# Depthwise convolution: the shifted copies of a chunk's quarters by DMA within SBUF instead of products with the identity

## The chip, the cores and the metric

One core of a Trainium2 chip runs the whole program. The metric is the device time of one execution in microseconds, as the median of several runs; lower is better. Engine names are those of the profile: PE (matmuls) and PEld (its weight loads), DVE, ACT, POOL, and SP, whose queue issues nearly all DMAs.

## The reference

Two layers on 256 tokens of 2048 channels in float32. Layer 0 mixes tokens by a state-space model, layer 1 by a convolution module; each mixer is followed by a SwiGLU FFN, and each half ends in a residual and a LayerNorm. The change lies in the convolution module of layer 1:

```python
CONV_WIDTH = 31
def conv_mixer(u, w_pw1, w_dw, b_dw, g_norm, b_norm, w_pw2):
    d = u.shape[-1]
    ab = u @ w_pw1
    v = ab[..., :d] * jax.nn.sigmoid(ab[..., d:])
    v = lax.conv_general_dilated(            # causal, one filter of 31 taps per channel
        v, w_dw[:, None, :], window_strides=(1,), padding=((CONV_WIDTH - 1, 0),),
        dimension_numbers=('NWC', 'WIO', 'NWC'), feature_group_count=d) + b_dw
    v = layer_norm(v, g_norm, b_norm)
    return jax.nn.silu(v) @ w_pw2
```

## The kernel before, in words

Activations lie with channels on the 128 partitions, in 16 chunks of 128 channels. The first product of the module (`cv_w_pw1`) runs in 8 panels, i = 0 to 7; a panel makes two chunks, `ch = 2 * i` and `2 * i + 1`. A panel has 4 units. A unit is 512 rows of the weights, loaded by SP into one of 4 `raw` buffers (L572, two DMAs for a unit of these panels), split by ACT (`whi`, L816) and DVE (`wlo`, L817) into one of 2 pairs of buffers, and used by 24 matmuls of 128x512 (L870; in the last panel 48 of 128x256, L874). The same 4 `raw` buffers also take the weights of the conditioning projection (`rawa`, L670), 0.6 of a 1 MB load for each unit, which DVE multiplies and adds (`adaacc`, L685).

The order around the products is set by two counters. `later.put(n, fn)` traces `fn` n units later, ahead of that unit's matmuls; `turning.put` does the same for the transposes that follow a panel. The units of the panels are units 1 to 32 of the count used here: panel i has 4i+1 to 4i+4. The framework then orders each engine's queue by its own estimate of what is ready, so the order on the chip is near, but not always equal to, the order of tracing. Each engine runs its queue strictly in order.

A panel's gated output is turned back to channels-on-partitions by 4 transposes (`turned`, L886) in unit 4i+6, that is in the second unit of the next panel. Panel 0 (made by another routine) and panel 7 need no such turn. Then `conv_in(i)` runs:

- ACT copies each chunk behind 30 zeros into one of two `pad` tiles (L1497).
- POOL makes the tap weights `lw` (L1502), three buffers, one for each chunk.
- `conv_spread` (L1513): the 128 channels of a chunk are four quarters q of 32. For each quarter, 4 products with 32 columns of the identity put it on the partitions 32j to 32j+31, moved by j = 0..3 positions, into one PSUM bank of 284 columns; ACT (q even, L1515) or DVE (q odd, L1517) copies the bank into `vs`. So `vs[32j + c, q, t]` is channel 32q + c at position t + j.
- `conv_out` (L1523): 8 tap groups x 4 quarters of products of `lw` (128 x 32) with `vs` (128 x 256) give a chunk's convolution; DVE moves it to `V` with the bias (L1527, L1532), and the sums for the LayerNorm are kept (`cstats.add`, L750 to L761).

The spread of chunk k (0 or 1) of a panel is put off by 1 + k units, its `conv_out` by 2 + k. After panel 7 all that was put off is worked off (`later.flush()`, L1540), the LayerNorm's sums are finished (L776 to L795), and the second product (`cv_w_pw2`) starts.

Of the kernel before, what the change touches and what calls it, by code (L numbers as in the profile page):

```python
# [11 lines left out]
F32 = mybir.dt.float32  # L12
# [7 lines left out]
P = 128  # L20
# [125 lines left out]
def bc(ap, axis, n):  # L146

    a = ap.unsqueeze(axis)
    sh = list(a.shape)
    sh[axis] = n  # L150
    return a.broadcast_to(sh)
# [344 lines left out]
def kernel(  # L496
# [9 lines left out]
    nc = tc.nc  # L506
# [6 lines left out]
    def aux(name):  # L513
        return auxp.tile([P, 512], F32, tag="aux", name=name)
# [81 lines left out]
    later, turning = Later(), Later()  # L596
# [839 lines left out]
    with mctx:  # L1436
# [46 lines left out]
        cp = cvctx.enter_context(tc.tile_pool(name="cv", bufs=1, reuse_waits="tile"))  # L1483
        V = cp.tile([P, NCH, SEQ], F32, name="V")
        LP = WIDTH - 1 + SEQ + 1
        LS = 4 * CONV_G - 4 + SEQ
# [7 lines left out]
        def conv_in(i, t):  # L1494
            p = pad[i % 2]
            for k in range(2):
                nc.scalar.copy(out=p[:, k, WIDTH - 1:LP - 1].rearrange("p (c t) -> p t c", t=2), in_=t[:, k].rearrange("p (t c) -> p t c", t=2))  # L1497
            for k in range(2):
                ch = 2 * i + k
                vs = cp.tile([P, 4, LS], F32, tag="vs", name="vs", bufs=3)  # L1500
                lw = cp.tile([P, 4, CONV_G, 32], F32, tag="lw", name="lw", bufs=3)
                nc.gpsimd.tensor_tensor(  # L1502
                    out=lw, in0=fold32.unsqueeze(1).unsqueeze(1).broadcast_to([P, 4, CONV_G, 32]),
                    in1=bc(wtap[:, :, 4 * ch:4 * ch + 4].rearrange("p g q -> p q g"), 3, 32), op=MUL)
                later.put(1 + k, lambda z=p[:, k], vs=vs: conv_spread(z, vs))
                later.put(2 + k, lambda ch=ch, lw=lw, vs=vs: conv_out(ch, vs, lw))

        def conv_spread(z, vs):

            for q in range(4):  # L1510
                b = aux("spread")[:, :LS]
                for j in range(4):
                    nc.tensor.matmul(b[32 * j:32 * j + 32, :], ident[:, 32 * q:32 * q + 32], z[:, j:j + LS], start=True, stop=True)  # L1513
                if q % 2 == 0:
                    nc.scalar.copy(out=vs[:, q], in_=b)  # L1515
                else:
                    nc.vector.tensor_copy(out=vs[:, q], in_=b)  # L1517

        def conv_out(ch, vs, lw):
            acc = aux("conv")[:, :SEQ]  # L1520
            for g in range(CONV_G):
                for q in range(4):
                    nc.tensor.matmul(  # L1523
                        acc[32 * q:32 * q + 32, :], lw[:, q, g, :], vs[:, q, 4 * g:4 * g + SEQ], start=g == 0, stop=g == CONV_G - 1)
            o, a = V[:, ch].rearrange("p (t c) -> p c t", t=2), acc.rearrange("p (c t) -> p c t", t=2)
            if ch < 2:
                nc.vector.tensor_scalar(out=o, in0=a, scalar1=cb_col[:, ch:ch + 1], scalar2=None, op0=ADD)  # L1527
                if ch == 1:
                    later.put(1, lambda: cstats.begin(V[:, 0:2]))
                    later.put(1, lambda: cstats.add(0, V[:, 0:2]))  # L1530
                return
            nc.vector.scalar_tensor_tensor(  # L1532
                out=o, in0=a, scalar=cb_col[:, ch:ch + 1], in1=cstats.shift.rearrange("p (t c) -> p c t", t=2), op0=ADD, op1=SUB)
            if ch % 2 == 1:
                cstats.add(ch // 2, V[:, ch - 1:ch + 1])

        for i in range(8):
            gated(cv_w_pw1[0], 256 * i, D, sp, lambda t, i=i: conv_in(i, t), entry if i == 0 else None, wp=wp, wide=i < 7,
                  ahead=(cv_w_pw2[0], [(0, 512)]) if i == 7 else None)
# [87 lines left out]
```

## Time and profile before

| | |
|---|---|
| median of 3 runs | 2364.49 us (2362.25 to 2364.72) |
| the profiled execution's own time | 2360.99 us |
| its span | 2359.0 us |
| mean granted TensorE clock | 0.989 |
| PE busy | 2278.7 us (97%) |
| DVE busy | 1647.2 us (70%) |
| ACT busy | 1024.3 us (43%) |
| POOL busy | 235.8 us (10%) |
| DMA, mean | 243 GB/s |

The span is the stretch that the profile covers; the times quoted are counted from its start. The panels of `cv_w_pw1` that follow panel 0 run from about 1207 to 1452 us, and the flush ends at about 1470 us. A row of a timeline gives start, duration, engine, line, operation, output and inputs, and a count when several were merged; in square brackets is how long the engine was idle before and what ended that. A row of the chain gives start, duration and work; the chain is followed back from the last instruction to what released each step. A row of stretches gives, for each engine, busy us and number of instructions, then PE's granted clock, the busy share of the 16 DMA engines and their rate in GB/s.

### The profile page before, as it was taken

To read this page: it belongs to the slowest core of one execution; us is meant where nothing else is said; L and a number is where in the kernel's file an instruction comes from. 1 tells how busy PE (TensorE), PEld (TensorE's weight loads), DVE (VectorE), ACT (ScalarE), POOL (GpSimd) and SP (SyncE) were. 2 spreads that over 40 slices of the span, in tenths; PEclk is the share of its full clock that TensorE was granted. 3 is DMA by queue.
4 is the path that set the end of the run, shared out by engine and by line. 5 is a ranking of instruction groups with operands and counts; after the bars stand their busy time and mean duration, and the time that the engine had idled before them with its cause. 6 is when DMAs were issued, how large, how long until landed. Compare 5 with 4: busy or idle time off the path is not lost.

```text
span 2359.0 us, 34477 instructions
## 1 busy us (share of the span) xinstructions
PE 2278.7 (97%) x14109; PEld 1817.0 (77%) x14109; DVE 1647.2 (70%) x1818; ACT 1024.3 (43%) x1267; POOL 235.8 (10%) x290
## 2 busy tenths in 40 slices
PE   6888999999999999999999999899999999999999
PEld 2455778888888888888977666788888888888888
DVE  7899988877776777778885554788755454555464
ACT  4666335643433333334463232557334333343443
POOL 2673000200000000000041111402000000000000
PEclk9999999999999999999999999999999999999999
DMA  9987799488888888888744553775775555555542
GB/s 325 327 282 246 262 337 337 160 294 324 298 316 300 319 304 307 303 313 293 268 160 161 196 198 112 265 252 174 268 236 192 184 191 187 188 192 183 190 160 98
DMA packets 369332, 572.17 MB, mean 243 GB/s; under 512 B 13043, under 2 KB 263203, under 8 KB 354451
## 3 DMA queue, kind: packets, MB, share of 16 engines
q1 hardware_dynamic: 368582, 568.48, 69.9%
q8 instruction: 110, 1.80, 0.3%
q10 hardware_dynamic: 400, 1.13, 0.2%
q0 software_dynamic: 192, 0.37, 0.1%
q14 instruction: 48, 0.39, 0.0%
HBM read 567.83 MB, written 2.10 MB: 242 GB/s over the span
## 4 chain that ended last, share of the span: by engine, by line
PE 78%; DVE 8%; issue 6%; POOL 3%; ACT 3%; DMA 2%; ACTq 0%; DVEq 0%; SPq 0%; POOLq 0%
PE acc L870 66%; PE acc L874 4%; PE conv L1523 2%; PE turned L886 2%; DMA raw<-in_s_w_glu_dram 1%; PE spread L1513 1%; DVE wlo L817 1%; ACT whi L816 1%; POOL h L968 1%; DVE pin L452 1%; PE y L489 1%; DMA nat<-in_s_b_re_dram 1%; DVE adaacc L685 1%; DVE x L440 0%; DVE pin L440 0%
## 5 line engine op out<-in xcount | busy, mean ns | idle before, releaser
L817 DVE TENSOR_TENSOR wlo<-raw,whi 128x2048 fp32r<-128x2048 f32 x344 | 790.7, 2299 | 526.7 <-ACT whi L816 526.6
L816 ACT CAST whi<-raw 128x2048 fp32r<-128x2048 f32 x344 | 655.0, 1904 | 822.9 <-PE acc L870 598.9
L870 PE MATMUL acc<-whi,h 128*128 128x512 f32 x3648 | 901.3, 396 | 12.5 <-ACT whi L816 11.1
L870 PEld LDWEIGHTS acc<-whi,h 128*128 128x128 f32 x3648 | 680.6, 189 | 175.5 <-ACT whi L816 16.6
L870 PE MATMUL acc<-wlo,h 128*128 128x512 f32 x1824 | 464.6, 392 | 0.2
L870 PEld LDWEIGHTS acc<-wlo,h 128*128 128x128 f32 x1824 | 342.4, 188 | 76.4 <-DVE wlo L817 1.1
L870 PE MATMUL acc<-whi,f 128*128 128x512 f32 x1248 | 300.5, 391 | 0.0
L685 DVE SCALAR_TENSOR_TENSOR adaacc<-rawa,c_act,adaacc 128x2048 f32<-128x2048 f32 (+1 forms) x135 | 284.7, 2109 | 0.4
L870 PEld LDWEIGHTS acc<-whi,f 128*128 128x128 f32 x1248 | 233.0, 188 | 48.9 <-ACT whi L816 0.8
L870 PE MATMUL acc<-wlo,f 128*128 128x512 f32 x624 | 156.4, 389 | 0.0
L870 PEld LDWEIGHTS acc<-wlo,f 128*128 128x128 f32 x624 | 117.1, 188 | 24.3
L1502 POOL TENSOR_TENSOR lw<-fold,wtap 128x1024 f32<-128x1024 f32 x16 | 41.8, 2620 | 894.2 <-PE acc L874 710.5
L615 PE MATMUL ada<-raw,c_rep 128*32 128x512 f32 x512 | 73.6, 655 | 10.9 <-DMA raw<-in_ada_w_dram 7.7
L968 POOL TENSOR_TENSOR h<-hf,h 128x512 fp32r<-128x512 f32 x24 | 48.1, 2015 | 329.9 <-ACT h L967 322.7
L1193 ACT ACTIVATE fsg<-acc 128x256 f32<-128x256 f32 x84 | 31.9, 380 | 102.5 <-PE acc L870 102.4
L1139 POOL CAST lnmh<-lno 128x2 fp32r<-128x2 f32 x1 | 0.2, 182 | 713.5 <-DVE lno L65 713.5
L874 PEld LDWEIGHTS acc<-h,whi 128*128 128x128 f32 x512 | 62.5, 192 | 7.7 <-DVE h L1552 3.0
L874 PE MATMUL acc<-h,whi 128*128 128x256 f32 x512 | 66.3, 285 | 2.1 <-DVE h L1552 1.3
L1523 PE MATMUL conv<-vs,lw 128*32 128x256 f32 x1024 | 61.4, 381 | 0.4 <-DVE vs L1517 0.3
L1523 PEld LDWEIGHTS conv<-vs,lw 128*32 128x32 f32 x1024 | 33.0, 110 | 25.6 <-issue 4.5
L1194 DVE TENSOR_TENSOR fsg<-acc,fsg 128x256 f32<-128x256 f32 x84 | 35.3, 420 | 19.9 <-ACT fsg L1193 19.8
L452 DVE TENSOR_TENSOR_SCAN pin<-rho,pin 128x256 f32<-128x256 f32 x64 | 44.4, 693 | 1.5
(336 smaller groups left out, 1894.8 us busy)
## 6 DMA issues: line engine op xcount, KB each, us to landing
raw<-in_ffn_w_gu_dram SPq DMA_DIRECT2D x352, 512.0 KB, 4.3
rawa<-in_ada_w_dram SPq DMA_DIRECT2D x128, 1024.0 KB, 5.3
raw<-in_ffn_w_down_dram SPq DMA_DIRECT2D x88, 1024.0 KB, 5.0
raw<-in_ada_w_dram SPq DMA_DIRECT2D x64, 1024.0 KB, 7.2
raw<-in_s_w_glu_dram SPq DMA_DIRECT2D x64, 512.0 KB, 5.8
raw<-in_cv_w_pw_dram SPq DMA_DIRECT2D x64, 512.0 KB, 4.8
raw<-in_cv_w_pw_dram SPq DMA_DIRECT2D x16, 1024.0 KB, 5.3
X<-in_x_dram SPq DMA_DIRECT2D x8, 256.0 KB, 11.3
```

Source lines behind the costliest of these rows:

```text
L452: v.tensor_tensor_scan(out=z, data0=rh[:, a].rearrange("p r h c -> p (r h c)"), data1=z, initial=0.0, op0=MUL, op1=ADD)
L615: nc.tensor.matmul(acc[32 * k:32 * k + 32, :], c_rep[:, 4 * u + k, :], r[:, k, :], start=u == 0, stop=u == 3)
L685: nc.vector.scalar_tensor_tensor(out=acc, in0=r[:, i], scalar=c_act[:, kk:kk + 1], in1=acc, op0=MUL, op1=ADD)
L816: m1 = nc.scalar.copy(out=self.hi[:, :kn], in_=r[:, :kn])
L817: m2 = nc.vector.tensor_tensor(out=self.lo[:, :kn], in0=r[:, :kn], in1=self.hi[:, :kn].bitcast(F32), op=SUB)
L870: nc.tensor.matmul(acc[bank].rearrange("p a b -> p (a b)"), x[:, bank * HALF:(bank + 1) * HALF], wt[:, k], start=first, stop=end)
L874: nc.tensor.matmul(acc[bank][:, i], wt[:, k, m * P:(m + 1) * P], x, start=first and i == 0, stop=end and i == 1)
L886: nc.tensor.transpose(b[:, o:o + HALF], u[t][:, c0 + k * P:c0 + (k + 1) * P], ident)
L968: nc.gpsimd.tensor_tensor(out=hl[:, s2], in0=h, in1=hh[:, s2].bitcast(F32), op=SUB)
L1194: nc.vector.tensor_tensor(out=t[:, i], in0=gv[:, 0], in1=t[:, i], op=MUL)
L1502: nc.gpsimd.tensor_tensor(out=lw, in0=fold32.unsqueeze(1).unsqueeze(1).broadcast_to([P, 4, CONV_G, 32]), in1=bc(wtap[:, :, 4 * ch:4 * ch + ...
L1523: nc.tensor.matmul(acc[32 * q:32 * q + 32, :], lw[:, q, g, :], vs[:, q, 4 * g:4 * g + SEQ], start=g == 0, stop=g == CONV_G - 1)
```

## The change

For panels 0 to 6 `vs` holds both chunks of a panel (two buffers instead of three of half the size), and 16 DMAs on SP's queue, traced 3 units after `conv_in`, copy from `pad` to `vs` what the identity products made; `conv_out` follows 5 + k units after `conv_in` instead of 2 + k. Panel 7 keeps its products, their place, and the place of its `conv_out`.

```diff
+            vs = cp.tile([P, 2, 4, LS], F32, tag="vs", name="vs", bufs=2)
+            if i < 7:
+                later.put(3, lambda: conv_copies(p, vs))
             for k in range(2):
                 ch = 2 * i + k
-                vs = cp.tile([P, 4, LS], F32, tag="vs", name="vs", bufs=3)
                 lw = cp.tile([P, 4, CONV_G, 32], F32, tag="lw", name="lw", bufs=3)
...
-                later.put(1 + k, lambda z=p[:, k], vs=vs: conv_spread(z, vs))
-                later.put(2 + k, lambda ch=ch, lw=lw, vs=vs: conv_out(ch, vs, lw))
+                if i == 7:
+                    later.put(1 + k, lambda k=k: conv_spread(p[:, k], vs[:, k]))
+                later.put((2 if i == 7 else 5) + k, lambda ch=ch, k=k, lw=lw: conv_out(ch, vs[:, k], lw))
+
+        def conv_copies(p, vs):
+
+            for j in range(4):
+                for q in range(4):
+                    nc.sync.dma_start(vs[32 * j:32 * j + 32, :, q], p[32 * q:32 * q + 32, :, j:j + LS])
```

## The prediction

> **What bounds the kernel now.** I read the page's busy shares and chain first, to see whether an engine or a chain of waits sets the time.
>
> ```profile
> span 2359.0 us, 34477 instructions
> PE 2278.7 (97%) x14109; PEld 1817.0 (77%) x14109; DVE 1647.2 (70%) x1818; ACT 1024.3 (43%) x1267; POOL 235.8 (10%) x290
> ...
> PE acc L870 66%; PE acc L874 4%; PE conv L1523 2%; PE turned L886 2%; DMA raw<-in_s_w_glu_dram 1%; PE spread L1513 1%; DVE wlo L817 1%; ACT whi L816 1%; POOL h L968 1%; DVE pin L452 1%; PE y L489 1%; DMA nat<-in_s_b_re_dram 1%; DVE adaacc L685 1%; DVE x L440 0%; DVE pin L440 0%
> ```
>
> PE is the bound, and the products that the change takes away (spread, L1513) are themselves 1% of the chain. An average over the span says nothing about the stage, so next come the stretches of four panels, cut from one `turned` to the next.
>
> ```profile
> 1289.27:1323.57 34.30, 34.30 (x294) 24.01 (x293) 19.72 (x16) 11.17 (x14) 5.98 (x2) 1.00 0.55 177
> 1323.57:1358.32 34.75, 34.63 (x294) 23.91 (x293) 19.69 (x16) 11.17 (x14) 4.73 (x2) 1.00 0.59 200
> 1358.32:1393.07 34.75, 34.64 (x295) 23.91 (x293) 21.72 (x17) 11.18 (x14) 6.77 (x2) 1.00 0.58 198
> 1393.07:1427.33 34.26, 34.26 (x319) 25.02 (x317) 19.75 (x16) 11.16 (x14) 5.99 (x2) 1.00 0.54 177
> ```
>
> The columns are length, then busy us of PE, PEld, DVE, ACT and POOL, the granted clock, the DMA share and GB/s. PE is busy for all but 0.1 us of a panel at clock 1.00; DVE has 13 us to spare, ACT 23, the DMA engines 40%. Here a microsecond of PE work is a microsecond of time, until something else binds. The chain through one of these panels shows what it is made of (start, us, what):
>
> ```profile
> 1289.27 0.44 PE turned L886 x4
> 1289.70 5.52 PE acc L870 x24
> 1295.22 2.05 PE spread L1513 x32
> 1297.28 5.71 PE acc L870 x24
> 1302.98 3.59 PE conv L1523 x64
> 1306.57 1.97 PE spread L1513 x32
> 1308.55 5.72 PE acc L870 x24
> 1314.26 3.59 PE conv L1523 x64
> 1317.85 5.71 PE acc L870 x24
> 1323.57 0.44 PE turned L886 x4
> ```
>
> The reader is to see that nothing but PE stands in it.
>
> **What goes.** Each of 14 chunks (panels 0 to 6) loses one group of 32 spread records. Two groups take 2.05 + 1.97 = 4.02 us of a panel, so seven panels lose 28.1 us. The stretches of the whole stage, restricted to L1513, put an upper bound on it:
>
> ```profile
> sum 253.00, PE 37.36 PEld 15.78; mean PE 4.15 PEld 1.75
> ```
>
> These 37.36 us are for 16 chunks and count overlap with the neighbouring groups; 14/16 of it is 32.7. I take 28.1, the chain's own time. The 28 evictions each on ACT and DVE go as well; both engines have the spare time shown, so I count nothing for them.
>
> **What comes: 16 copies a panel on SP and the DMA engines.** No transfer within SBUF is in this trace, so the price is bounded by other rows: SP's issues of loads, their landing, and the part of the schedule around one panel's `conv_in`.
>
> ```profile
> L572 SPq DMA_DIRECT2D raw<-in_cv_w_pw_dram x80: 367/368/1223, 1155.0 to 1556.5; - x80
> L572 SPq DMA_DIRECT2D raw<-in_ada_w_dram x64: 367/368/3095, 3.3 to 1478.6; - x64
> DMA to landing us min/median/max: 3.3/4.7/15.9
> 1285.55 0.92 SPq L572 DMA_DIRECT2D raw<-in_cv_w_pw_dram  x2
> 1289.74 0.67 ACT L1497 COPY pad<-turned 128x256 f32<-128x256 f32 x2 [0.32 <-PE turned L886]
> 1301.19 1.90 ACT L816 CAST whi<-raw 128x2048 fp32r<-128x2048 f32 x1 [3.93 <-PE acc L870]
> ```
>
> (min/median/max of the issue in ns; the third row is from issue to landing.) Issue: a load takes 0.37 us of SP, whether for one segment or for four rows of it, so 16 copies take 5.9 us; the upper bound is 3.10 us each, the lower one nothing. I take 0.37, the row's median. Bytes: a copy has 32 partitions x 2 x 284 x 4 = 72.7 KB in 64 rows of 1136 B, 16 of them 1.16 MB. The DMA engines moved 200 GB/s at a share of 0.59, so 339 GB/s when busy: 3.4 us a panel. With the 0.59 x 34.75 = 20.5 us that they have now, 23.9 of a panel of 30.5 (34.5 less 4.0). So DMA doesn't bind.
>
> The Trainium skill says less well of such copies: "SBUF — State Buffer" (The DMA setup-cost knee) has a transfer of 64 KiB at about 138 GB/s, and in its section on the port swizzle 32 partitions reach only half of the ports. At 138 GB/s the estimate is 8.4 us a panel, 28.9 of the 30.5 us; the sum would still be PE's, with the queue nearly full. No run here shows it yet.
>
> Who waits behind the copies: SP runs in order, and the copies of panel i are traced ahead of the load for unit 4i+9. For panel 2 that load, unit 17's, was issued at 1285.55 (whi at 1301.19), and `pad` is written at 1289.74 + 0.67 = 1290.41. In strict order SP is held 4.9 us for `pad` and 5.9 us for the copies, 10.8 us in all. In the new order, with both conv groups in units 15 and 16, unit 17 starts at 1289.71 + 5.5 + 2 x (3.59 + 5.71) = 1313.8. Its whi must start by 1311.9, so with 0.92 us of issue and 4.7 us to land the load may leave SP at 1306.3: 20.7 us of hold are free, 10.8 are used. Cost nothing; if a copy held SP for over (20.7 - 4.9)/16 = 1.0 us, PE would begin to wait.
>
> Who waits for the copies: `conv_out` is now 5 units after `conv_in`, and `pad` to conv is some 5.0 + 5.7 + 5.7 + 5.7 us and two earlier conv groups, over 29 us, against 5.9 us of issue and 4.7 us to land. Cost nothing in panels 1 to 6. The last copies (panel 6) also have room: `pad` is there two and a half units and two conv groups before panel 7 ends.
>
> Semaphores on PE: a matmul that waits for several transfers needs waiting instructions in its queue.
>
> ```profile
> L1523 PEldq EVENT_SEMAPHORE  x13: 51/51/51, 1275.3 to 1463.8; - x13
> ```
>
> If each of 112 copies is waited for by one, 112 x 0.051 = 5.7 us; if the waits hide behind the streaming of matmuls, nothing. I take the middle, 2.9.
>
> **The start.** Here the conv work of panel 0 was filler while units were made ready.
>
> ```profile
> 1224.07 3.61 POOL L968 TENSOR_TENSOR h<-hf,h 128x512 fp32r<-128x512 f32 x2 [4.67 <-issue]
> 1227.11 2.73 DVE L817 TENSOR_TENSOR wlo<-raw,whi 128x2048 fp32r<-128x2048 f32 x1 [0.59 <-ACT whi L816]
> 1230.66 0.44 ACT L1497 COPY pad<-sg 128x256 f32<-128x256 f32 x1
> ```
>
> Unit 8's inputs are there at 1227.7 (POOL) and 1229.8 (wlo), so PE can do units 8 and 9 from 1227.7 to 1239.1. The copies can't start before the second chunk is in `pad`, 1231.1; with 5.9 us of issue and 4.7 us to land, `vs` is whole at 1241.7. If `conv_out` stands ahead of unit 9 (as traced) PE waits 1241.7 - 1233.4 = 8.3 us, behind it 2.6 us, behind unit 10 nothing. I take 2.6, as groups do move by readiness in this trace (the conv of panel 0 ran ahead of unit 8).
>
> **The end.** After panel 7's products:
>
> ```profile
> 1452.17 3.59 PE conv L1523 x64
> 1455.76 1.98 PE spread L1513 x32
> ...
> 1464.45 4.23 PE conv L1523 x64
> 1468.71 0.67 DVE V L1532
> 1469.40 0.70 DVE cln_s L759
> ```
> ```profile
> 1457.53 0.68 DVE L761 TENSOR_TENSOR cln_s<-cln_s,lnsq 128x512 f32<-128x512 f32 x1
> L1502 POOL TENSOR_TENSOR lw<-fold,wtap x16: 1967/2065/4024, 1181.3 to 1444.7; 128x1024 f32<-128x1024 f32 x16
> ```
>
> One conv group more stands here (chunk 12's and 13's, where 13's stood alone), moved from ahead of the last unit, so PE's sum is unchanged. Chunk 13 is traced last, and its sums need one more add on DVE (0.68) than panel 7's. The last `lw` waits for chunk 12's conv and takes POOL 2.07 to 4.02 us; chunk 14's conv (3.59) can cover it. In return 3 conv groups and 2 spread groups, 14.8 us, took 1452.17 to 1468.68 = 16.5 us, and the extra group can fill that gap. Bounds 1.7 us gained to 2.8 lost; I take 0.7 lost.
>
> **Sum.** 28.1 - 2.9 - 2.6 - 0.7 = 21.9 us off the profiled execution's own 2360.99 us: 2339.1. That execution stands 3.5 us below the median of the runs, which would give 2342.6; I say 2341.
>
> **Rivals.** (1) Partly uncovered: the waits at the start (8.3), the semaphores (5.7) and the end (2.8) all at their upper bound leave 28.1 - 16.8 = 11.3 us: 2350. For it: strict order at the start. Against: the list of PE's work in that stretch is already out of traced order.
> (2) SP holds the loads back: at 1.22 us a copy, the largest row of these loads, 19.5 us less the free 15.8 is 3.7 us a panel, some 26 us in seven: the gain is gone, 2361, no change. Against: 80 issues have 0.37 as median.
> (3) Slower: the copies pass one after another, each only when the one before has landed. At the smallest landing, 3.3 us, a panel needs 52.8 us for its `vs`, 18.3 more than 34.5 now, 128 us over seven panels: 2489. It decides from 34.5/16 = 2.16 us a copy. Against: the two issues of a unit at 1285.55 are both out in 0.92 us, while each takes 3.3 us or more to land, so transfers overlap. The fixed cost of roughly 2 us a transfer in the Trainium skill ("SBUF — State Buffer", The DMA setup-cost knee) would, paid in series, come to about 35 us a panel by estimate, which is no change; whether it is paid in series is what the traces decide.
>
> **How the numbers follow.** Forecast 0.70 (2331 to 2346), rival 1 0.12 (2346 to 2358), rival 2 0.07, rival 3 0.11. 2331 is 28.1 + 1.7 off 2361 with nothing lost. The range 2331 to 2358 takes in the forecast and rival 1. About 0.2%, 4.7 us, is what a measurement can tell from no change. Faster 0.82, same 0.07, slower 0.11.
>
> **What would show it.** Right: panels of 30.3 to 31 us with PE busy throughout, L1513 down to 64 records, 112 issues on SP of some 0.37 us each, whi waiting on PE and not on DMA. Wrong: PE or PEld idle until a DMA into `vs` (rivals 1 and 3), or whi until a DMA into `raw` (rival 2); issues well above 1 us; a gap of PE near 1235.

## The result and the profile after

Medians of the runs: 2349.6 us (2346.0 to 2352.6) against 2364.6 us (2362.25 to 2369.67) for the kernel before, ratio 0.9932, 95% interval 0.9917 to 0.9947. A fourth execution, the profiled one, took 3188.87 us at a granted clock of 0.654 and is left out, so the profile shown here is that of a second series ("again", the same kernel). That series came to 2356.57 us against 2365.81, ratio 0.9941 (0.992 to 0.9963). The change makes the kernel faster, by 9 to 15 us, which is 0.6 to 0.7%; 21.9 us were forecast.

From the page of again: span and busy time.

```profile
span 2355.0 us, 33652 instructions
...
PE 2263.1 (96%) x13661; PEld 1820.4 (77%) x13661; DVE 1643.5 (70%) x1790; ACT 1013.4 (43%) x1239; POOL 228.7 (10%) x290
```

The span mixes the changed stage with everything else, so I cut the stage out: from the first product of panel 0 (L985) to the first product of the LayerNorm's sums (L776). First the kernel before, then again (columns as in the prediction: length, busy us of PE, PEld, DVE, ACT, POOL with their counts, granted clock, DMA share, GB/s).

```profile
1181.10:1470.20 289.10, 282.56 (x2577) 205.40 (x2576) 174.40 (x174) 111.53 (x155) 57.44 (x24) 1.00 0.50 166
```
```profile
1189.00:1465.10 276.10, 259.41 (x2130) 204.04 (x2129) 169.72 (x146) 100.65 (x127) 50.01 (x24) 0.99 0.66 203
```

Length less PE's busy time is PE's idle time: 6.5 us before, 16.7 after. The stage is 13.0 us shorter, although PE has 23.2 us less to do. The rest of the span was 2069.9 us before and 2078.9 here; over all thirteen kernels of this study it lies between 2070 and 2084 with no relation to the copies. So causes are read from the stage of one execution, and times from the medians.

The parts of the change in again, instructions by line and tile:

```profile
L1522 PE MATMUL spread<-pad,ident x64: 400/402/427, 1443.9 to 1452.0; 128*32 128x284 f32 x64
L1532 PEldq EVENT_SEMAPHORE  x39: 51/51/51, 1249.1 to 1454.4; - x39
L1515 SPq DMA_DIRECT2D vs<-pad x112: 585/595/1626, 1238.8 to 1441.6; - x112
DMA to landing us min/median/max: 2.0/2.5/10.2
```

The 64 spread records of panel 7 are left, and 112 copies stand on SP's queue, as forecast. But a copy takes 0.595 us to issue, not 0.37. One panel in the timeline of again:

```profile
1288.60 1.15 SPq L572 DMA_DIRECT2D raw<-in_cv_w_pw_dram  x2
1289.84 15.68 SPq L1515 DMA_DIRECT2D vs<-pad  x16
1299.91 1.90 ACT L816 CAST whi<-raw 128x2048 fp32r<-128x2048 f32 x1 [7.32 <-DMA vs<-pad]
1301.86 2.12 PE L870 MATMUL acc<-whi,h 128*128 128x512 f32 x8 [0.32 <-ACT whi L816]
1305.62 1.14 SPq L572 DMA_DIRECT2D raw<-in_cv_w_pw_dram  x2
1305.88 1.21 PE L870 MATMUL acc<-wlo,h 128*128 128x512 f32 x4 [1.90 <-DVE wlo L817]
1307.40 2.51 SPq L572 DMA_DIRECT2D raw<-in_cv_w_pw_dram  x4
```

The group of 16 holds SP from 1289.84 to 1305.52, and the loads behind it then leave all together. PE's two waits here, 0.32 and 1.90 us, have another source: the load ahead of the group (1288.60) lands only at 1299.81, whi starts late, and wlo after it. (The bracket of whi names a copy, but whi reads `raw` alone.) The chain through that load:

```profile
1288.60 0.37 SPq L572
...
1289.01 10.79 DMA raw<-in_cv_w_pw_dram
```

It left as soon as a wlo had freed its buffer (1288.57), so it did not itself stand behind copies, and it took 10.8 us to land. That wlo was late on two counts: its own load, issued at 1269.84 behind the group of the panel before, had landed only at 1280.83, and DVE had been idle for 4.25 us until 1280.94, waiting for a convolution to end. More on the second under once5.

In the waits of again from 1225 to 1460 (total us, times, longest), the engines first, then SP's queue:

```profile
ACT whi L816 <- DMA raw<-in_cv_w_pw_dram: 62.3, 14, 7.8
...
PE acc L870 <- ACT whi L816: 5.8, 3, 2.8
...
PE acc L870 <- DVE wlo L817: 4.0, 3, 1.9
```
```profile
SPq L572 <- DVE wlo L817: 43.0, 9, 11.0
...
SPq L1515 <- DMA raw<-in_cv_w_pw_dram: 17.7, 10, 4.5
```

whi waiting for a DMA into `raw` is the sign that the prediction set for rival 2. The last line is a thing it didn't consider: a copy inside the group waits for an earlier load to land. In the group above, the seventh and the eighth copy leave at 1296.27 and 1299.82; the two DMAs of the load at 1288.60, each eight places ahead in SP's queue, land at 1296.25 and 1299.81. So the holds of panels 1 to 6 are 11.5, 15.7, 13.5, 13.4, 13.4 and 15.1 us, mean 13.8, where 16 bare issues would be 9.5.

### The profile page after: what moved, and what is told of

Same layout as the page of the kernel before. It is cut to its first block, busy times and chain, and to the rows that moved or that the text cites. A ratio compares the mean times of both kernels' runs of the same rounds, so it can differ in the third digit from the quotient of the medians.

```text
span 3187.1 us, 33652 instructions
## 1 busy us (share of the span) xinstructions
PE 3151.7 (99%) x13661; PEld 2085.7 (65%) x13661; DVE 1647.1 (52%) x1790; ACT 1015.4 (32%) x1239; POOL 226.0 (7%) x290
## 4 chain that ended last, share of the span: by engine, by line
PE 96%; DVE 1%; POOL 1%; DMA 1%; ACT 1%; issue 0%; ACTq 0%; DVEq 0%; POOLq 0%
PE acc L870 75%; PE acc L874 6%; PE acc L985 3%; PE conv L1532 3%; PE turned L886 2%; PE ada L615 1%; PE y L489 1%; PE pin L423 0%; DMA nat<-in_s_b_re_dram 0%; PE adar L693 0%; PE out L1119 0%; POOL mu L313 0%; PE adat L622 0%; PE xt L1288 0%; DMA nat<-in_s_c_im_dram 0%
## 5 line engine op out<-in xcount | busy, mean ns | idle before, releaser
L870 PE MATMUL acc<-whi,h 128*128 128x512 f32 x3648 | 1253.6, 510 | 0.7 <-ACT adas L618 0.7
L870 PEld LDWEIGHTS acc<-whi,h 128*128 128x128 f32 x3648 | 754.5, 208 | 429.0 <-issue 141.8
L870 PE MATMUL acc<-wlo,h 128*128 128x512 f32 x1824 | 647.3, 507 | 0.0
L870 PEld LDWEIGHTS acc<-wlo,h 128*128 128x128 f32 x1824 | 377.6, 207 | 217.4 <-issue 72.6
L870 PE MATMUL acc<-whi,f 128*128 128x512 f32 x1248 | 426.5, 509 | 0.0
L870 PEld LDWEIGHTS acc<-whi,f 128*128 128x128 f32 x1248 | 258.3, 208 | 145.6 <-issue 46.9
L870 PE MATMUL acc<-wlo,f 128*128 128x512 f32 x624 | 220.6, 508 | 0.0
L870 PEld LDWEIGHTS acc<-wlo,f 128*128 128x128 f32 x624 | 129.5, 207 | 74.6 <-issue 25.2
L615 PE MATMUL ada<-raw,c_rep 128*32 128x512 f32 x512 | 97.3, 864 | 4.3 <-DVE c_rep L561 3.2
L1193 ACT ACTIVATE fsg<-acc 128x256 f32<-128x256 f32 x84 | 31.9, 380 | 188.7 <-PE acc L870 188.7
L1532 PE MATMUL conv<-vs,lw 128*32 128x256 f32 x1024 | 91.7, 511 | 0.0
L874 PE MATMUL acc<-f,whi 128*128 128x256 f32 x320 | 54.9, 345 | 0.0
```

The lines of the kernel that those rows point to most:

```text
L615: nc.tensor.matmul(acc[32 * k:32 * k + 32, :], c_rep[:, 4 * u + k, :], r[:, k, :], start=u == 0, stop=u == 3)
L870: nc.tensor.matmul(acc[bank].rearrange("p a b -> p (a b)"), x[:, bank * HALF:(bank + 1) * HALF], wt[:, k], start=first, stop=end)
L874: nc.tensor.matmul(acc[bank][:, i], wt[:, k, m * P:(m + 1) * P], x, start=first and i == 0, stop=end and i == 1)
L1532: nc.tensor.matmul(acc[32 * q:32 * q + 32, :], lw[:, q, g, :], vs[:, q, 4 * g:4 * g + SEQ], start=g == 0, stop=g == CONV_G - 1)
```

## The experiments

The theory: taking the products away is worth what was forecast, and SP's queue gives part of it back, since the loads that feed PE stand behind the copies. Rivals: the copies' data come late for `conv_out`; the new place of `conv_out` costs time; the DMA engines are the limit; the loss is in the granted clock or elsewhere in the span; the framework gives PE's queue another order ("Order" in the expectation of again). "Stage", "PE idle" and the granted clock of the stage are read as above, from one execution each.

| kernel | ratio to before (95%) | stage, us | PE idle in it, us | clock |
|---|---|---|---|---|
| before | 1 | 289.1 | 6.5 | 1.00 |
| again | 0.9941 (0.992 to 0.9963) | 276.1 | 16.7 | 0.99 |
| once5 | 0.9867 (0.9839 to 0.9895) | 258.0 | 7.2 | 1.00 |
| once2 | 0.9884 (0.9862 to 0.9906) | 258.2 | 6.4 | 1.00 |
| both | 1.0003 (0.9988 to 1.0018) | 288.8 | 6.9 | 1.00 |
| idle5 | 0.9946 (0.9929 to 0.9963) | 275.5 | 18.9 | 0.99 |
| pool | 0.9906 (0.9889 to 0.9923) | 263.6 | 8.6 | 0.99 |
| actq | 0.992 (0.9902 to 0.9938) | 269.3 | 13.0 | 0.98 |
| spaced | 1.0019 (1.0005 to 1.0034) | 289.3 | 25.3 | 0.99 |
| idle8 | 0.9884 (0.9863 to 0.9905) | 259.3 | 6.5 | 0.99 |
| thin16 | 0.9908 (0.9887 to 0.993) | 263.2 | 9.5 | 0.99 |
| two8 | 0.9954 (0.9938 to 0.997) | 279.8 | 17.1 | 0.97 |
| mix | 0.988 (0.9858 to 0.9902) | 258.5 | 7.6 | 1.00 |

**again**: the changed kernel, nothing edited.

> The changed kernel once more, for an undisturbed profile. Three theories for the 8 us or so that are missing against the 21.9 forecast. Order: the framework expects the copies late and queues the conv groups in pieces between units; then PE is busy, no engine waits for a copy, but the two conv groups take more than 7.2 us a panel. Loads: a copy's issue takes 0.59 us where 0.37 was forecast, so SP is held 9.5 us a panel and whi waits for raw; then ACT's whi is seen waiting for a DMA, and PE for whi. Clock: the stage is as short as forecast (about 22 us less) and the rest of the kernel is longer at a lower granted clock. All expect 2346 to 2353.

The extra idle time lies in this stage (6.5 to 16.7 us). Of the 9.5 us by which it exceeds once5's, 6.5 are waits of the L870 products for whi and wlo and 2.5 are waits of the transposes.

**once5**: copies in panel 0 alone; panels 1 to 6 convolve its `vs`.

```diff
+        kept = []
...
-            vs = cp.tile([P, 2, 4, LS], F32, tag="vs", name="vs", bufs=2)
-            if i < 7:
+            vs = kept[0] if 0 < i < 7 else cp.tile([P, 2, 4, LS], F32, tag="vs", name="vs", bufs=2)
+            if i == 0:
+                kept.append(vs)
                 later.put(3, lambda: conv_copies(p, vs))
```

> The 16 copies are made for panel 0 alone, and panels 1 to 6 convolve panel 0's copies (their own are left out); conv_out stays 5 units after conv_in. Order and loads both expect the missing time back, since the conv groups stay whole in the queue and SP carries 16 copies instead of 112: 2364 - 28 + 1 to 4 for start and end, 2337 to 2340. Clock expects no more than 3 us off the changed kernel, 2346 to 2350.

2337.37 us. The stage, and the chain through one panel:

```profile
1186.80:1444.80 258.00, 250.83 (x2134) 194.03 (x2134) 165.67 (x146) 100.60 (x127) 53.78 (x24) 1.00 0.57 190
```
```profile
1278.93 0.44 PE turned L886 x4
1279.37 5.51 PE acc L870 x24
1284.88 3.59 PE conv L1535 x64
1288.47 5.72 PE acc L870 x24
1294.18 3.59 PE conv L1535 x64
1297.78 11.21 PE acc L870 x48
1308.98 0.44 PE turned L886 x4
```

This is the panel that the prediction drew: 30.05 us, nothing but PE in the chain. The stage is 31.1 us shorter than before, so the copies of panels 1 to 6 cost 18.1 us in again: 9.5 of PE's idle time and 8.6 of longer busy time, for the same number of products. At most 3.4 is the clock: again's stage has two stretches of 3.41 us at a granted clock of 0.50 (1229.77 and 1403.85), once5's has none. Another part is in these groups of PE (busy us, mean ns of one, idle us before), in again and then in once5:

```profile
L1532 PE MATMUL conv<-vs,lw 128*32 128x256 f32 x1024 | 62.8, 380 | 0.0
...
L886 PE MATMUL turned<-ident,sg 128*128 128x128 f32 x24 | 4.8, 288 | 2.5 <-DVE sg L1048 2.5
```
```profile
L1535 PE MATMUL conv<-vs,lw 128*32 128x256 f32 x1024 | 59.7, 380 | 0.0
...
L886 PE MATMUL turned<-ident,sg 128*128 128x128 f32 x24 | 3.6, 274 | 0.0
```

Together they are 6.8 us more in again, and the order of PE's queue is not the same. In once5 each convolution stands whole between units, as in the chain above. In again most of a panel's two convolutions stand right behind the transposes, and the rest in small pieces (10 products in 1.05 us at 1322.68, where a whole 64 take 3.66 in once5). The chain of again shows what such a block does to DVE's queue:

```profile
1343.54 7.25 PE conv L1532 x128
...
1350.82 0.70 DVE V L1541
...
1353.38 2.29 DVE wlo L817
```

The whi for this wlo was done at 1346.66, but wlo stands behind `V`, which waits for the whole block, and PE then waits 1.05 us for wlo. So a part of the loss goes with the order that the framework chose once the copies stood on SP's queue, and not with late loads alone.

**once2**: once5, with `conv_out` back at 2 + k for panels 1 to 6.

```diff
-                later.put((2 if i == 7 else 5) + k, lambda ch=ch, k=k, lw=lw: conv_out(ch, vs[:, k], lw))
+                later.put((5 if i == 0 else 2) + k, lambda ch=ch, k=k, lw=lw: conv_out(ch, vs[:, k], lw))
```

> As the run before, but conv_out of panels 1 to 6 is back at 2 units after conv_in. It separates the later place of conv_out from the copies: if the later place costs something at the end (one conv group more behind the last unit, one add more), this is 1 to 3 us shorter than the run before, else the same within 1 us. Order and loads: 2335 to 2340. Clock: 2346 to 2350.

258.2 us of stage against 258.0: the place of `conv_out` by itself costs nothing.

**both**: the kernel before, its products kept, with 112 copies that nobody reads (and two `lw` buffers, for room).

```diff
+            vx = cp.tile([P, 2, 4, LS], F32, tag="vx", name="vx", bufs=1)
+            if i < 7:
+                later.put(3, lambda: conv_copies(p, vx))
...
-                lw = cp.tile([P, 4, CONV_G, 32], F32, tag="lw", name="lw", bufs=3)
+                lw = cp.tile([P, 4, CONV_G, 32], F32, tag="lw", name="lw", bufs=2)
...
```

> The kernel before, with its identity products, and the 112 copies beside them into a tile that nobody reads (two buffers for lw instead of three make room). Order expects no change, 2364 within 3 us, since no conv group waits for a copy. Loads expects a loss, since SP is held as in the changed kernel: 2368 to 2380. Clock expects 2364 to 2372, by a lower clock if copies lower it.

No difference. Its stage:

```profile
1186.60:1475.40 288.80, 281.94 (x2579) 205.59 (x2579) 174.27 (x174) 110.92 (x155) 50.63 (x24) 1.00 0.61 195
```

The copies alone are free where a panel takes 34.5 us; here their groups held SP for 10.2 to 12.7 us, and PE's queue keeps the order that it has before. The slack that hides the copies is partly made of the very time that the change saves. The row also prices the bytes: 0.61 x 288.8 less 0.50 x 289.1 is 31.6 us of the DMA engines, some 4.5 for each panel's copies.

**idle5**: once5, with the copies of panels 1 to 6 made as in the changed kernel, but into a tile that no product reads (the edit is against the changed kernel).

```diff
-            vs = cp.tile([P, 2, 4, LS], F32, tag="vs", name="vs", bufs=2)
+            vs = cp.tile([P, 2, 4, LS], F32, tag="va" if i == 0 else "vs", name="vs", bufs=1)
             if i < 7:
-                later.put(3, lambda: conv_copies(p, vs))
+                later.put(3, lambda vs=vs: conv_copies(p, vs))
+            if i == 0:
+                kept.append(vs)
+            if 0 < i < 7:
+                vs = kept[0]
```

> Panels 1 to 6 make their 16 copies, but into a tile that nobody reads; their conv_out reads panel 0's copies (so the later panels convolve the wrong chunk). Hold (SP is held by the 16 issues of 0.59 us and by the waits among them, so the loads of weights behind them leave late): as the changed kernel, 2347 to 2357, with whi waiting for raw. Dependence (conv_out waits for its copies): as with the copies of panel 0 alone, 2335 to 2341. Bytes (the copies' 1.16 MB a panel crowd the DMA engines): 2347 to 2357.

275.5 us of stage, 0.6 less than again. The loss is there though no product waits for a copy; with once2 this takes the data dependence and the place of `conv_out` out. Here the chain passes through SP's queue itself:

```profile
1363.57 7.53 DMA raw<-in_cv_w_pw_dram
...
1371.11 0.58 SPq L1521
...
1380.61 10.72 DMA raw<-in_cv_w_pw_dram
...
1391.64 1.76 DVE wlo L817
```

A load lands at 1371.10, the copy eight places behind it leaves, eight more copies follow it, then the loads, and the last of these is waited for by wlo. That is the hold. But idle5's PE queue has an order like again's in every panel, so this run doesn't tell the hold from the order.

**pool, actq**: all copies from another queue.

```diff
-                    nc.sync.dma_start(vs[32 * j:32 * j + 32, :, q], p[32 * q:32 * q + 32, :, j:j + LS])
+                    nc.gpsimd.dma_start(vs[32 * j:32 * j + 32, :, q], p[32 * q:32 * q + 32, :, j:j + LS])
```

(actq: `nc.scalar`.)

> The changed kernel with its copies issued from POOL's queue instead of SP's, same place in the trace. Hold: SP is free, whi no longer waits for raw, the missing time comes back: 2336 to 2342. Bytes: the same bytes cross the same DMA engines, 2347 to 2357. Dependence: between, by how late POOL issues; if POOL takes over 1 us a copy, conv_out waits at the start only, 2340 to 2348.

> The same with ACT's queue. Hold: SP is free but ACT, which makes whi, is held 9.5 us a panel; with 23 us to spare a panel some of the time comes back, 2339 to 2350. Bytes: 2347 to 2357. Dependence: 2347 to 2357.

pool: 2344.22 us. This is the run that tells the queue from the DMA engines. The landing of the loads (L572) from 1260 to 1440 us in again, then in pool:

```profile
DMA to landing us min/median/max: 3.9/7.0/11.9
```
```profile
DMA to landing us min/median/max: 3.8/7.1/13.8
```

In both, loads land late beside the copies (4.8 us median before, in the same stretch). In pool PE is idle for 0.01 us of these 180 all the same; in again for 9.8. So late landing by itself isn't what PE pays for. SP's queue in pool:

```profile
SPq L572 <- DVE wlo L817: 80.1, 15, 17.6
```

Its loads wait for their buffer to come free, 80.1 us in all against 43.0 in again, and leave as soon as it is. PE's queue in pool has once5's order from panel 1 on. The 5.6 us by which pool's stage exceeds once5's lie at the start: two stretches of 3.41 us at a granted clock of 0.50 (1225.71 and 1253.02), worth at most 3.4, and a wait for panel 0's copies, which are urgent:

```profile
PE conv L1532 <- DMA vs<-pad: 2.2, 1, 2.2
```

A copy issued by POOL takes 0.536 us to issue and 6.9 us (median) to land. The Trainium skill says of issuing from several engines ("DMA: Bandwidth & Descriptors", Issuing engines are not separate DMA queues) that it saves only the sequencer's issue time, usually small beside the transfer. The DMA engines are indeed shared here, for the loads land as late beside POOL's copies as beside SP's (7.1 and 7.0 us). But what counted was the queue that the copies stand in, because the same queue issues the loads. On ACT's queue (2348.28 us) the cost moves to where ACT makes whi:

```profile
ACT whi L816 <- DMA vs<-pad: 33.6, 4, 12.7
```

**spaced**: the 16 copies in four groups of four, 1 to 4 units after `conv_in`.

```diff
-                later.put(3, lambda: conv_copies(p, vs))
+                for j in range(4):
+                    later.put(1 + j, lambda j=j: conv_copies(p, vs, j))
...
```

> The changed kernel with its 16 copies traced as four groups of 4 (one j each), 1 to 4 units after conv_in, instead of all at 3. Hold: no stretch over 2.4 us plus a wait is taken at once, most of the time comes back: 2339 to 2348. Bytes: no change, 2347 to 2357. Dependence: copies start earlier, the last is one unit later, 2345 to 2357.

A miss: 2370.79 us, the whole gain lost. Its SP waits from 1225 to 1460:

```profile
SPq L1515 <- ACT pad L1497: 36.3, 7, 10.2
```

The first group reaches SP before `pad` is written and stands there for 36.3 us in all, loads behind it. That is the hold again, longer and for another reason, and the convolutions are broken into still more pieces (their products are busy for 66.6 us); the experiment doesn't show what spacing alone would do.

**idle8, thin16**: idle5 with 8 copies a panel in panels 1 to 6, and with 16 copies of one chunk each (half the bytes).

```diff
-                later.put(3, lambda vs=vs: conv_copies(p, vs))
+                later.put(3, lambda vs=vs: conv_copies(p, vs, 2 if i else 4))
...
-            for j in range(4):
+            for j in range(nj):
...
```
```diff
-                later.put(3, lambda vs=vs: conv_copies(p, vs))
+                later.put(3, lambda vs=vs: conv_copies(p, vs, 1 if i else 2))
...
-                    nc.sync.dma_start(vs[32 * j:32 * j + 32, :, q], p[32 * q:32 * q + 32, :, j:j + LS])
+                    nc.sync.dma_start(vs[32 * j:32 * j + 32, :nk, q], p[32 * q:32 * q + 32, :nk, j:j + LS])
```

> As the run with unread copies, but 8 of the 16 in panels 1 to 6 (j 0 and 1 alone); the later panels again convolve panel 0's copies. Number (SP is held by the count of issues, 0.59 us each, and by the wait of the ninth and later ones for an earlier transfer): SP is held 4.7 us a panel and no copy waits within its group, most of the 17.6 us between 257.9 and 275.5 us of the stage comes back: stage 258 to 263, time 2337 to 2344. Bytes: half comes back, stage 266 to 268, time 2345 to 2349.

> As the run with unread copies, but each of the 16 copies takes one of the two chunks, so 16 issues with half the bytes. Number: the issues hold SP as before if an issue's price does not go with the rows: stage 272 to 276, time 2350 to 2357. Bytes: half comes back, stage 266 to 268, time 2345 to 2349. If an issue gets cheaper with 32 rows instead of 64, number expects that share back too.

Over once5's stage, 8 copies cost 1.3 us, 16 thin ones 5.2, 16 whole ones (idle5) 17.5. The longest hold of idle8 and two of thin16 from their timelines:

```profile
1278.11 8.97 SPq L1521 DMA_DIRECT2D vs<-pad  x8
```
```profile
1313.52 11.10 SPq L1521 DMA_DIRECT2D vs<-pad  x16
1345.22 11.02 SPq L1521 DMA_DIRECT2D vs<-pad  x16
```

The same bytes cost 1.3 us in 8 copies and 5.2 in 16; the same number costs 5.2 with half the bytes and 17.5 with all. Neither count nor bytes alone is the measure, and the numbers that I had set for thin16 fell. The hold orders these cases: 5.1 to 9.0 us of SP (idle8) cost nearly nothing, 10.7 to 12.0 (thin16) 5.2 us, 11.4 to 15.6 (idle5) 17.5. But the order of PE's queue sorts them too: thin16 and idle8 have once5's from the third set of transposes on, idle5 nowhere. With once5's order, a hold of 11 us costs nothing: the two panels of thin16 that begin at 1311.1 and 1341.2, with the holds shown, take 30.1 us each. The 5.2 us are in part a wait of 2.34 us of the transposes for `sg` (1373.86) and at most 1.7 of clock (3.41 us at 0.50, at 1373.96). No run has a longer hold in that order.

**two8**: two groups of eight, 3 and 4 units after `conv_in`, `conv_out` one unit later.

```diff
-                later.put(3, lambda: conv_copies(p, vs))
+                for j in range(4):
+                    later.put(3 + j // 2, lambda j=j: conv_copies(p, vs, j))
...
-                later.put((2 if i == 7 else 5) + k, lambda ch=ch, k=k, lw=lw: conv_out(ch, vs[:, k], lw))
+                later.put((2 if i == 7 else 6) + k, lambda ch=ch, k=k, lw=lw: conv_out(ch, vs[:, k], lw))
...
```

> The changed kernel with its copies in two groups of 8 (j 0 and 1, then j 2 and 3) traced 3 and 4 units after conv_in, and conv_out at 6 units plus k, one later. Number: a hold is 4.7 us instead of 9.5, the loads get in between, and no copy waits for one of its own group: stage 260 to 268, time 2339 to 2349. Bytes: no change, stage 274 to 278, time 2349 to 2357.

Another miss: 279.8 us of stage. Its SP waits:

```profile
SPq L1515 <- DMA raw<-in_cv_w_pw_dram: 20.2, 13, 3.1
```

Copies waited for loads 13 times (10 in again), now that loads stand between the groups. Its granted clock in the stage was 0.97 (17.1 us at 0.50, worth at most 8.5 us), so PE's idle time (also 17.1 us) is the safer figure: splitting did not help. Its convolutions stand in blocks like again's.

**mix**: panel 0's copies on SP, those of panels 1 to 6 on POOL.

```diff
-                later.put(3, lambda: conv_copies(p, vs))
+                later.put(3, lambda: conv_copies(p, vs, nc.gpsimd if i else nc.sync))
...
-                    nc.sync.dma_start(vs[32 * j:32 * j + 32, :, q], p[32 * q:32 * q + 32, :, j:j + LS])
+                    eng.dma_start(vs[32 * j:32 * j + 32, :, q], p[32 * q:32 * q + 32, :, j:j + LS])
```

> The changed kernel with panel 0's copies on SP, where they are needed soonest, and those of panels 1 to 6 on POOL's queue. Hold on SP by the number of issues: SP carries 16 copies as in the run that copies panel 0 alone, so about that time: stage 258 to 262, time 2337 to 2343, the fastest kernel with the right copies. Bytes: 2344 to 2357.

2337.38 us (2333.75 to 2339.26), faster than the kernel before and, its interval lying below, than the changed one. Its stage:

```profile
1180.20:1438.70 258.50, 250.94 (x2130) 194.11 (x2129) 168.35 (x146) 100.31 (x127) 102.84 (x120) 1.00 0.74 217
```

258.5 us with every copy made and read, where once5 has 258.0 without those of panels 1 to 6, at a DMA share of 0.74, higher than again's 0.66. PE's queue has once5's order again. It computes the whole reference and is the version to keep.

## Why the prediction was partly right

The sign and the range held, but 2349.6 (and 2356.6) lie above the forecast's own 2331 to 2346. They are in the band of rival 1, whose waits (start, semaphores, end) did not come: the loss came behind the copies on SP's queue, where rival 2 had looked for it, at 18.1 of rival 2's some 26 us. That the range held is luck in part. It was made wide for rival 1, and the forecast's terms erred both ways: the gain and the small losses were better than forecast by some 9 us, and a term put at nothing cost more than that. By its steps:

- *What goes* (28.1 us): once5's stage is 31.1 us shorter. The spread records went from 37.4 us to 5.5, which is 31.9: the upper bound of the prediction (32.7) was nearer than the chain's 4.0 us a panel. By their records the two groups of panel 0 took 5.4 us, and those of panels 1 to 6 4.4 a panel.
- *Semaphores* (2.9): the waits on PE's queue went from 13 to 39, at 0.051 us 1.3.
- *The start* (2.6) and *the end* (0.7): in once5, which has both, PE is idle 0.6 us more than before. A gap near 1235 is not there.
- *Bytes* (3.4 us of the DMA engines a panel): 4.5. The estimate from the Trainium skill ("SBUF — State Buffer", The DMA setup-cost knee), 8.4 us, was too high; the measured number decides. As forecast, the DMA engines don't bind: pool and mix move the same bytes without the loss.
- *Who waits for the copies* (nothing): held, by idle5 and once2.
- *Rival 3* (serial copies): fell. 16 copies leave within 11.5 to 15.7 us and land in 2.5 us each (median).
- *Who waits behind the copies*: "Cost nothing". This is the step that failed; in again it cost 18.1 us, of which at most 3.4 are clock. The issue was sized by a load (0.37) and is 0.595, so that 5.9 us became 9.5; waits inside the group, which had no term, made it 13.8. That is still less than the 20.7 us held to be free, so the slack was wrong as well. It was worked out for a single load landing in 4.7 us, in the order of the kernel before. Beside the copies the median of the landing is 7.0, the loads behind a group leave in a bunch, and PE's queue came out in another order, in which wlo stands behind whole blocks of convolutions. In the prediction's unit, 0.86 us a copy already lost 18 us, where it put the point at 1.0.

Without that step its sum errs to the safe side: it had 21.9 us, and mix, with the copies of panels 1 to 6 out of SP's way, has a stage 30.6 us shorter than before. That its 2337.38 us stand only 3.6 from the forecast 2341 is partly the choice of the base: beside mix the kernel before took 2367.19.

Shown by the runs: that the removal is worth its full price, that the loss comes with copies on SP's queue and not from their data, their bytes or late landing alone, and that it goes when they are moved. Not settled: how the 18.1 us divide between the hold of SP (issue, waits inside the group, bunching of loads) and the new order of PE's and DVE's queues, since moving the copies changed both; about 6.8 us go directly with the order of PE's queue. A run with again's copies and once5's order of PE's queue would tell. Nor is it settled whether smaller groups on SP could be placed so that they cost nothing, as spaced and two8 both met other waits.

## What to carry to other kernels

When DMA replaces work of a bound engine, first ask whose queue issues it and what stands behind it there. Size the issue by a row of the same shape or not at all, add the waits inside a group, and compare the hold with the slack of the stage as it will be after the saving, for all the loads in flight and not for one. Then see whether the bound engine's queue kept its order. Copies that are not urgent go on the queue of an engine that feeds nobody; the few that are urgent stay on the fast one.

## What the hardware showed beside that

- A copy within SBUF of 64 rows of 1136 B takes 0.595 us to issue on SP, 0.607 on ACT and 0.536 on POOL (medians), more than a 512 KB load on SP in the kernel before (0.368). With half the rows it takes 0.507 at least; the median of thin16's 112 copies, 16 of them whole, is 0.589.
- From SP it lands in 2.5 us, from POOL in 6.9, both medians in the changed kernel's places.
- No DMA left its queue before the one eight places ahead in that queue had landed: none of the 152 on SP in again (1225 to 1445 us) for which the trace tells the landing, none of 109 on POOL in pool; of the one seven places ahead 18 and 26 did not wait. Copies waited so for loads 10 times on SP in again (17.7 us) and for other copies 13 times on POOL in pool (17.0 us).
